# Attention: asking for q and k of the next pair of heads ahead of v of the next four heads

## The chip, the cores and the metric

The kernel runs on one core of one Trainium2 chip. The metric is the device time of one execution in microseconds (us), the median of several runs; lower is better. The engines are named as the profile names them: PE (TensorE, the matrix engine), PEld (its weight loads), DVE (VectorE), ACT (ScalarE), POOL (GpSimd) and SP (SyncE, which here issues the transfers).

## What is computed

One layer of a streaming encoder on 1024 frames of width 1024: a SwiGLU, a mixer with two branches (a gated spatial MLP and an attention), and a second SwiGLU. The change is in the attention, whose 16 heads of width 64 weigh the frames by stick breaking:

```python
z = jnp.einsum('bhtd,bhsd->bhts', qb, kb).astype(jnp.float32) * scale
causal = s_idx < t_idx
log_keep = jnp.where(causal, -jax.nn.softplus(z), 0.0)
log_w = jax.nn.log_sigmoid(z) + lax.cumsum(log_keep, axis=3, reverse=True) - log_keep
w = jnp.where(causal, jnp.exp(log_w), 0.0)
outs.append(jnp.einsum('bhts,bhsd->bhtd', w.astype(vb.dtype), vb))
```

q, k and v are columns of one projection `h @ w_in` of the normed input.

## The kernel before

Each factor of a matmul is kept as two parts, a rounded one and the rest, and a product is three matmuls (lines 67 to 69, `mm3`). A scheduler sets the order on each engine: it takes the instructions in the order in which the program asks for them as their priority, and puts a later one in front when an earlier one has to wait for an operand or for a free buffer. So the order of the calls in `attention` is a ranking, and each engine then runs its own fixed list.

The attention goes through eight pairs of heads. Three kinds of work meet in it:

- `head` (16 times): for each block b of 128 query frames, two matmuls into `z` for up to 512 key frames each (L572, L573), two sigmoids on ACT into `kp` and `bt`, a mask on POOL (L581), a running product on DVE from right to left over `kp` (the scan, L583), a product into `bt` on POOL or DVE (L587), transposes on PE (`tr`, L600), their split into two parts on ACT and DVE (`wt`, L73 and L74), and the product with v (`av`, L607). `kp` has 3 buffers, so block b+3 of a head waits until block b is through.
- `proj_qk` (8 times, once for a pair of heads): q in two halves of 512 frames, then k in two halves, each half 24 matmuls of 512 columns into a PSUM tile `pj` (L67 to L69). Each half of q is then copied into q of the pair's first head and of its second head, the rounded part on ACT and the rest on DVE (`q<-pj`). Tiles `q`, `kh` and `kl` have 3 buffers each, one for a head.
- `proj_v` (4 times, once for four heads, a "group" here): eight products of 24 matmuls of 256 columns into a PSUM tile `pv`, each split into a tile `v`.

`pj` and `pv` are both taken from the PSUM tag `p1`, which has two buffers; the other tags (`p0` with 3 for z, `p2` with 2 for tr, `p3` with 1 for av) hold the other six of the eight banks:

```python
bufs = {"p0": 3, "p1": 2, "p2": 2, "p3": 1}[tag]
```

Heads are numbered 0 to 15, pairs 0 to 7, groups 0 to 3 (heads 0 to 3 are group 0).

Of the kernel before, what the change touches and what calls it, by code (L numbers as in the profile page):

```python
# [32 lines left out]
class Kernel:  # L33
# [483 lines left out]
    def attention(self, ap, ydram):  # L517
        nc, w_in = self.nc, self.a["w_in"][0]

        def proj_v(quad):  # L520
            units = [self.load_cols(w_in, C_VV + quad * 256, kt0, 4, 256) for kt0 in (0, 4)]
            vt = []
            for t in range(NT):
                if quad == 0 and t and self.pending:
                    self.pending.pop(0)()
                half, c = t // 4, (t % 4) * P
                ps = self.psum("p1", "pv")
                for k in range(NK):
                    wh, wl = units[k // 4]
                    hh, hl = (self.h[half][part][:, k, c:c + P] for part in range(2))  # L530
                    self.mm3(ps[:, :256], hh, hl, wh[:, k % 4, :], wl[:, k % 4, :], k == 0, k == NK - 1)
                pool = ap if quad % 2 else self.gp
                v = pool.tile([P, 4, 2, HD], F32R, tag="v", bufs=8, name="v")
                self.split(v[:, :, 0, :], v[:, :, 1, :], ps[:, :256].rearrange("p (h d) -> p h d", h=4))
                vt.append(v)
            return vt

        def proj_qk(pair):
            lo, hi = slice(0, HD), slice(HD, P)
            kl = [ap.tile([P, S], F32R, tag="kl", bufs=3, name="kl") for _ in range(2)]  # L540
            q = [ap.tile([P, S], F32R, tag="q", bufs=3, name="q") for _ in range(2)]
            kh = [ap.tile([P, S], F32R, tag="kh", bufs=3, name="kh") for _ in range(2)]
            wh, wl = self.load_cols(w_in, C_Q + pair * P)
            for half in range(2):
                cs = slice(half * HALF, (half + 1) * HALF)
                ps = self.proj_t("p1", wh, wl, half)
                for e, (own, other) in enumerate(((lo, hi), (hi, lo))):
                    self.split(q[e][own, cs], q[e][other, cs], ps[own, :])
            wh, wl = self.load_cols(w_in, C_K + pair * P)
            for half in range(2):  # L550
                cs = slice(half * HALF, (half + 1) * HALF)
                ps = self.proj_t("p1", wh, wl, half)
                for e, (own, other) in enumerate(((lo, hi), (hi, lo))):
                    self.split(kh[e][own, cs], kl[e][own, cs], ps[own, :])
                    for k in (kh[e], kl[e]):
                        nc.sync.dma_start(out=k[other, cs].bitcast(F32), in_=k[own, cs].bitcast(F32))
            return [(q[e], kh[e], kl[e]) for e in range(2)]
# [62 lines left out]
        qk = {0: proj_qk(0)}  # L620
        npair = NHEAD // 2
        for pair in range(npair):
            for e in range(2):
                head(2 * pair + e, *qk[pair][e], vts[pair // 2])
            if pair % 2 == 1 and pair + 1 < npair:
                vts[pair // 2 + 1] = proj_v(pair // 2 + 1)
            if pair + 1 < npair:
                qk[pair + 1] = proj_qk(pair + 1)


    def gmlp(self, bs):
# [246 lines left out]
```

## Time and profile before

| | |
|---|---|
| median of 3 runs | 2537.75 us (2537.24 to 2537.94) |
| the profiled execution, its own time | 2535.71 us |
| its span, first to last instruction | 2534.0 us |
| busy over the span: PE, PEld, DVE | 2449.6, 2074.1, 1683.1 us |
| busy over the span: ACT, POOL | 1045.2, 351.7 us |
| mean granted clock of PE | 0.986 of full speed |

The span is what the rows below are counted in; the execution's own time is 1.71 us more. Busy time of PE overstates its work, since matmuls are pipelined and one row reaches into the next; the distance from one start to the next is what a matmul takes of PE's time.

### The profile page before, as it was taken

What the parts mean: (1) busy time and instruction counts of PE and PEld (TensorE: products, weight loads), DVE (VectorE), ACT (ScalarE), POOL (GpSimd) and SP (SyncE); (2) the same over time, 40 slices, a digit from 0 to 9 for tenths busy, and PEclk for the clock granted to TensorE, in tenths of its full rate; (3) what the DMA queues carried; (4) which work ended last, traced back from release to release, by engine and by line L of the source; (5) the groups of instructions that cost most, each with busy time, mean ns of one, the idle gap of its engine ahead of it and who ended that gap; (6) DMA issues with size and microseconds to landing.
All of it is one profiled execution on the core that took longest, in us unless ns stands there. A gap on an engine that the chain in (4) does not pass through costs nothing.

```text
span 2534.0 us, 33359 instructions
## 1 busy us (share of the span) xinstructions
PE 2449.6 (97%) x12268; PEld 2074.1 (82%) x12268; DVE 1683.1 (66%) x2579; ACT 1045.2 (41%) x1996; POOL 351.7 (14%) x510
## 2 busy tenths in 40 slices
PE   6999999999999999999999999999979999999998
PEld 5788888788888888888888888888857888887886
DVE  5877787565747888786675555155838777774655
ACT  6333333344545666665422222222334333333444
POOL 4000000000214544444300000000130000000002
PEclk9999999999999999999999999999989999999999
DMA  4553553775421212122121122133445535537653
GB/s 147 175 177 124 176 178 125 292 248 183 159 57 44 67 51 76 46 72 58 39 56 53 47 88 75 58 104 125 133 125 182 174 123 176 181 127 288 235 182 133
DMA packets 257636, 326.73 MB, mean 129 GB/s; under 512 B 15680, under 2 KB 172864, under 8 KB 257472
## 3 DMA queue, kind: packets, MB, share of 16 engines
q1 hardware_dynamic: 257472, 324.60, 39.5%
q8 instruction: 96, 1.57, 0.3%
q14 instruction: 68, 0.56, 0.1%
HBM read 231.74 MB, written 84.41 MB: 125 GB/s over the span
## 4 chain that ended last, share of the span: by engine, by line
PE 85%; DVE 6%; DMA 4%; issue 2%; ACT 2%; POOL 1%; SPq 0%; POOLq 0%; ACTq 0%; DVEq 0%
PE pj L67 7%; PE pj L68 7%; PE pj L69 7%; PE pd L168 7%; PE pd L167 7%; PE pd L166 7%; PE pb L167 5%; PE pb L168 5%; PE pb L166 5%; PE av L607 3%; PE tr L600 2%; PE pv L68 2%; PE pv L69 2%; PE pv L67 2%; PE pe L167 2%
## 5 line engine op out<-in xcount | busy, mean ns | idle before, releaser
L150 ACT CAST wf<-raw 128x512 fp32r<-128x512 f32 x280 | 166.6, 620 | 244.3 <-PE pd L168 108.8
L67 PE MATMUL pj<-h,wf 128*128 128x512 f32 x640 | 254.6, 398 | 5.4 <-DVE q L74 5.4
L151 DVE TENSOR_TENSOR wf<-raw,wf 128x512 fp32r<-128x512 f32 x264 | 177.9, 695 | 119.3 <-ACT wf L150 119.0
L68 PE MATMUL pj<-h,wf 128*128 128x512 f32 x640 | 254.2, 397 | 0.0
L69 PE MATMUL pj<-h,wf 128*128 128x512 f32 x640 | 253.4, 396 | 0.0
L583 DVE TENSOR_TENSOR_SCAN kp<-kp 128x128 f32<-128x128 f32 (+7 forms) x128 | 179.7, 1412 | 37.6 <-POOL kp L581 36.1
L57 DVE TENSOR_TENSOR wf<-raw,wf 128x1024 fp32r<-128x1024 f32 x88 | 110.2, 1252 | 128.5 <-ACT wf L56 128.4
L150 ACT CAST wf<-ws 128x512 fp32r<-128x512 f32 x176 | 108.0, 622 | 190.7 <-DVE ws L159 87.4
L56 ACT CAST wf<-raw 128x1024 fp32r<-128x1024 f32 x88 | 92.7, 1053 | 214.4 <-PE pj L68 117.9
L587 POOL TENSOR_TENSOR bt<-bt,kp 128x512 f32<-128x512 f32 (+4 forms) x128 | 130.3, 1021 | 130.5 <-DVE kp L583 98.0
L67 PEld LDWEIGHTS pj<-h,wf 128*128 128x128 f32 x640 | 122.3, 191 | 31.0 <-DVE q L74 6.8
L67 PE MATMUL pv<-wf,h 128*128 128x256 f32 x512 | 145.2, 286 | 2.5 <-ACT vg L650 2.1
L68 PE MATMUL pv<-wf,h 128*128 128x256 f32 x512 | 145.7, 285 | 0.3 <-DVE wf L57 0.3
L69 PE MATMUL pv<-wf,h 128*128 128x256 f32 x512 | 145.2, 284 | 0.0
L69 PEld LDWEIGHTS pj<-h,wf 128*128 128x128 f32 x640 | 122.0, 191 | 24.6 <-DVE wf L57 0.2
L68 PEld LDWEIGHTS pj<-h,wf 128*128 128x128 f32 x640 | 122.1, 191 | 24.0
L114 POOL TENSOR_TENSOR xn<-x,gain 128x512 f32<-128x512 f32 x12 | 16.7, 1391 | 893.2 <-DVE x L474 601.7
L166 PE MATMUL pb<-T,wf 128*128 128x512 f32 x352 | 137.4, 390 | 0.0
L167 PE MATMUL pb<-T,wf 128*128 128x512 f32 x352 | 137.2, 390 | 0.0
L168 PE MATMUL pb<-T,wf 128*128 128x512 f32 x352 | 136.8, 389 | 0.0
L167 PE MATMUL pd<-wf 128*128 128x512 f32 x344 | 134.7, 392 | 0.2 <-DVE wf L151 0.2
L166 PE MATMUL pd<-wf 128*128 128x512 f32 x344 | 132.8, 393 | 1.9 <-DVE x L463 1.4
(216 smaller groups left out, 6589.3 us busy)
## 6 DMA issues: line engine op xcount, KB each, us to landing
raw<-in_ff_w_down_dram SPq DMA_DIRECT2D x66, 512.0 KB, 6.2
raw<-in_w_in_dram SPq DMA_DIRECT2D x56, 512.0 KB, 3.8
raw<-in_ff_w_gate_dram SPq DMA_DIRECT2D x52, 512.0 KB, 4.3
raw<-in_ff_w_up_dram SPq DMA_DIRECT2D x44, 512.0 KB, 5.5
f_t2t<-as SPq DMA_DIRECT2D x22, 512.0 KB, 4.9
f_a11a<-act SPq DMA_DIRECT2D x44, 256.0 KB, 4.1
f_s2s<-as SPq DMA_DIRECT2D x22, 512.0 KB, 2.9
f_s3s<-as SPq DMA_DIRECT2D x22, 512.0 KB, 5.6
```

Of the source, the lines that this page charges most:

```text
L56: nc.scalar.copy(hi, raw)
L57: (nc.gpsimd if early else nc.vector).tensor_tensor(lo, raw, hi.bitcast(F32), op=ALU.subtract)
L67: mm(ps, lhsT=lh, rhs=rh, start=first, stop=False)
L68: mm(ps, lhsT=lh, rhs=rl, start=False, stop=False)
L69: mm(ps, lhsT=ll, rhs=rh, start=False, stop=last)
L150: self.nc.scalar.copy(f[:, 0, :], src)
L151: (sub or self.nc.vector.tensor_tensor)(f[:, 1, :], src, f[:, 0, :].bitcast(F32), op=ALU.subtract)
L166: mm(ps, lhsT=lh, rhs=rh, start=first, stop=False, skip_group_check=True)
L167: mm(ps, lhsT=lh, rhs=rl, start=False, stop=False, skip_group_check=True)
L168: mm(ps, lhsT=ll, rhs=rh, start=False, stop=last, skip_group_check=True)
L583: nc.vector.tensor_tensor_scan(rev, rev, rev, 1.0, op0=ALU.mult, op1=ALU.bypass)
L587: eng.tensor_tensor(bt[:, :n], bt[:, :n], kp[:, i * HALF + 1:i * HALF + 1 + n], op=ALU.mult)
```

## The change

The two calls at the end of a group change places; nothing else does. It concerns three places of the program, after heads 3, 7 and 11; at the ends of the other pairs only `proj_qk` is called.

```diff
@@ -622,10 +622,10 @@
         for pair in range(npair):
             for e in range(2):
                 head(2 * pair + e, *qk[pair][e], vts[pair // 2])
+            if pair + 1 < npair:
+                qk[pair + 1] = proj_qk(pair + 1)
             if pair % 2 == 1 and pair + 1 < npair:
                 vts[pair // 2 + 1] = proj_v(pair // 2 + 1)
-            if pair + 1 < npair:
-                qk[pair + 1] = proj_qk(pair + 1)
```

Every engine runs the same instructions as before, in another order: PE has 12,268 matmuls in both. The orders part at the end of `proj_qk` of pair 1, while head 1 runs, and what follows comes again with each group.

The first place is PE's list in the middle of head 2, at block 2 (`z_6785`). Before:

```order
L600 MATMUL tr_6553<-ident_66,bt_6537 128x128
L572 MATMUL z_6785<-kh_6608,q_6606 128x384
L573 MATMUL z_6785<-kl_6604,q_6606 128x384
L68 MATMUL pv_7358<-wf_7265,h00_81 128x256
L69 MATMUL pv_7358<-wf_7264,h01_82 128x256
L67 MATMUL pv_7358<-wf_7264,h00_81 128x256
L68 MATMUL pv_7358<-wf_7265,h00_81 128x256
L69 MATMUL pv_7358<-wf_7264,h01_82 128x256
```

And with the change, where `z_6798` and `z_6839` are blocks 3 and 4 of the same head:

```order
L600 MATMUL tr_6553<-ident_66,bt_6517 128x128
L572 MATMUL z_6785<-kh_6608,q_6606 128x384
L573 MATMUL z_6785<-kl_6604,q_6606 128x384
L572 MATMUL z_6798<-kh_6608,q_6606 128x512
L573 MATMUL z_6798<-kl_6604,q_6606 128x512
L600 MATMUL tr_6553<-ident_66,bt_6537 128x128
L600 MATMUL tr_6553<-ident_66,bt_6517 128x128
L600 MATMUL tr_6553<-ident_66,bt_6537 128x128
L607 MATMUL av_6437<-wt_6506,v_5858 128x256
L572 MATMUL z_6839<-kh_6608,q_6606 128x512
L573 MATMUL z_6839<-kl_6604,q_6606 128x512
```

The matmuls of v (`pv`) are gone from head 2; from its first z to the k of pair 2 PE has only 4 matmuls of a projection left among 113.

The second place is DVE's list in head 2 with the change: `q_7264` and `q_7265` are q of heads 4 and 5, `pj_7274` and `pj_7303` the two halves of q of pair 2 in the two buffers of `p1`, and `kp_6913` and `kp_6933` the scans of blocks 6 and 7 of head 2.

```order
L583 SCALAR_TENSOR_TENSOR kp_6913<-kp_6913 128x896
L74 TENSOR_TENSOR wt_6826<-tr_6822,wt_6826 128x384
L587 TENSOR_TENSOR bt_6923<-bt_6923,kp_6913 128x383
L74 TENSOR_TENSOR wt_6883<-tr_6878,wt_6883 128x512
L74 TENSOR_TENSOR q_7265<-pj_7274,q_7265 64x512
L74 TENSOR_TENSOR q_7265<-pj_7303,q_7265 64x512
L583 SCALAR_TENSOR_TENSOR kp_6933<-kp_6933 128x1024
```

Before, the same copies of pair 2 (there `q_7500` and `q_7501`) stood in head 3, each half's two together, behind the scan of its block 6 (`kp_7171`) for the second half:

```order
L583 SCALAR_TENSOR_TENSOR kp_7171<-kp_7171 128x896
L74 TENSOR_TENSOR wt_7084<-tr_7080,wt_7084 128x384
L57 TENSOR_TENSOR wf_8229<-raw_8226,wf_8228 128x1024
L587 TENSOR_TENSOR bt_7181<-bt_7181,kp_7171 128x383
L74 TENSOR_TENSOR wt_7141<-tr_7136,wt_7141 128x512
L74 TENSOR_TENSOR q_7500<-pj_7539,q_7500 64x512
L74 TENSOR_TENSOR q_7501<-pj_7539,q_7501 64x512
```

So with the change both buffers of `p1` are held from the first half of q, in head 1, to the end of head 2.

The third place is PE's list at the first z of head 4 (`z_7642`). Before, it stood right behind k of its pair (`pj_7607`):

```order
L67 MATMUL pj_7607<-h10_83,wf_7570 128x512
L68 MATMUL pj_7607<-h11_84,wf_7570 128x512
L69 MATMUL pj_7607<-h10_83,wf_7571 128x512
L572 MATMUL z_7642<-kh_7502,q_7500 128x128
L573 MATMUL z_7642<-kl_7498,q_7500 128x128
```

With the change the last product of v of the next group stands there:

```order
L67 MATMUL pv_7612<-wf_7412,h10_83 128x256
L68 MATMUL pv_7612<-wf_7413,h10_83 128x256
L69 MATMUL pv_7612<-wf_7412,h11_84 128x256
L572 MATMUL z_7642<-kh_7266,q_7264 128x128
L573 MATMUL z_7642<-kl_7262,q_7264 128x128
```

In front of it all of head 3 is through as well, where before a part of head 3's `tr` and `av` stood behind it.

## Rows read from the trace of the kernel before

**Rows 1.** The page: the span, and each engine's busy time over it.

```profile
span 2534.0 us, 33359 instructions
...
PE 2449.6 (97%) x12268; PEld 2074.1 (82%) x12268; DVE 1683.1 (66%) x2579; ACT 1045.2 (41%) x1996; POOL 351.7 (14%) x510
```

**Rows 2.** The attention: length; busy PE, PEld, DVE, ACT, POOL (count); clock, DMA share, GB/s.

```profile
738.00:1267.00 529.00, 510.42 (x3161) 455.47 (x3159) 406.46 (x460) 321.44 (x693) 234.25 (x384) 0.98 0.22 57
```

**Rows 3.** Timeline of PE: start, duration; in brackets the idle time before.

```profile
737.98 0.56 PE L572 MATMUL z<-kh,q 128*128 128x128 f32 x3
...
763.39 0.79 PE L67 MATMUL pj<-h,wf 128*128 128x512 f32 x1 [3.07 <-DVE q L74]
...
863.76 0.22 PE L572 MATMUL z<-kh,q 128*128 128x128 f32 x1
...
864.58 0.39 PE L67 MATMUL pj<-h,wf 128*128 128x512 f32 x1
...
888.72 0.87 PE L600 MATMUL tr<-ident,bt 128*128 128x128 f32 x3 [3.26 <-DVE wt L74]
...
892.39 0.50 PE L67 MATMUL pj<-h,wf 128*128 128x512 f32 x1 [0.23 <-DVE q L74]
...
989.01 0.31 PE L572 MATMUL z<-kh,q 128*128 128x128 f32 x1
...
1014.14 0.70 PE L600 MATMUL tr<-ident,bt 128*128 128x128 f32 x3 [1.50 <-DVE wt L74]
...
1015.87 0.80 PE L67 MATMUL pj<-h,wf 128*128 128x512 f32 x1 [1.02 <-DVE q L74]
...
1116.22 0.22 PE L572 MATMUL z<-kh,q 128*128 128x128 f32 x1
...
1142.09 0.80 PE L67 MATMUL pj<-h,wf 128*128 128x512 f32 x1 [1.09 <-DVE q L74]
```

**Rows 4.** Two stretches, columns as rows 2; then timeline of PE after the second.

```profile
888.10:891.50 3.40, 2.78 (x12) 2.81 (x13) 3.34 (x3) 2.57 (x8) 0.29 (x1) 0.50 0.66 200
1014.40:1021.20 6.80, 5.78 (x16) 4.22 (x15) 6.46 (x8) 0.84 (x3) 3.51 (x7) 0.50 0.15 31
...
1021.15 0.43 PE L67 MATMUL pj<-h,wf 128*128 128x512 f32 x1
```

**Rows 5.** DVE in the attention by line: busy, mean | idle, releasers; last: one shape.

```profile
L583 DVE TENSOR_TENSOR_SCAN kp<-kp 128x128 f32<-128x128 f32 (+7 forms) x128 | 179.7, 1412 | 37.6 <-POOL kp L581 36.1
L74 DVE TENSOR_TENSOR wt<-tr,wt 128x512 fp32r<-128x512 f32 (+1 forms) x160 | 98.0, 627 | 39.0 <-ACT wt L73 38.3
L587 DVE TENSOR_TENSOR bt<-bt,kp 128x127 f32<-128x127 f32 (+1 forms) x64 | 59.7, 932 | 11.0 <-POOL bt L581 8.3 <-DVE kp L583 0.5
L57 DVE TENSOR_TENSOR wf<-raw,wf 128x1024 fp32r<-128x1024 f32 x29 | 37.5, 1293 | 24.9 <-ACT wf L56 24.9
...
L74 DVE TENSOR_TENSOR q<-pj,q 64x512 fp32r<-64x512 f32 x32 | 21.8, 688 | 10.4 <-ACT q L73 9.8
L74 DVE TENSOR_TENSOR v<-pv,v 128x256 fp32r<-128x256 f32 x32 | 13.2, 412 | 13.2 <-ACT v L73 13.2
...
L583 DVE TENSOR_TENSOR_SCAN kp<-kp 128x1024 f32<-128x1024 f32 x16 | 36.7, 2291 | 1.5 <-POOL kp L581 1.4
```

**Rows 6.** Timeline of PE at full clock, at head 3.

```profile
866.77 0.99 PE L607 MATMUL av<-wt,v 128*128 128x256 f32 x7
867.60 0.93 PE L600 MATMUL tr<-ident,bt 128*128 128x128 f32 x7
868.29 0.48 PE L572 MATMUL z<-kh,q 128*128 128x512 f32 x1
868.60 0.39 PE L573 MATMUL z<-kl,q 128*128 128x512 f32 x1
868.83 0.39 PE L67 MATMUL pj<-h,wf 128*128 128x512 f32 x1
```

**Rows 7.** Transfers: size and median time to landing.

```profile
raw<-in_w_in_dram SPq DMA_DIRECT2D x56, 512.0 KB, 3.8
```

## Prediction

> **What bounds the kernel now.** I read the page's busy times first, then those of the attention alone, then PE's timeline at each idle row there. The span is 2534.0 us [rows 1] and the execution took 2535.71, 2.0 us under the median of 2537.75; a difference of the span is taken over to the median unchanged. From the first z the attention takes 529 us, with PE at 510 us of busy time, DVE at 406 us [rows 2]. So PE's list is nearly always running, DVE has room over the whole stretch, and the order counts for one thing: whether PE always has something ready while a head goes through its chain of ACT, POOL and DVE. Where it had not, PE's timeline shows it: four times, each between the first z of a head and the next matmul of `pj` that needs a buffer of `p1` [rows 3]. At heads 0, 4, 8 and 12 these stretches are 737.98 to 763.39 (25.4 us), 863.76 to 892.39 (28.6), 989.01 to 1015.87 (26.9) and 1116.22 to 1142.09 (25.9), and the wait that ends them is for DVE.
>
> **What the stretches lose.** PE's work in one is its matmuls by what one takes, start to start, at full clock [rows 6]: a matmul of 512 columns 0.23 us (868.60 to 868.83), seven `av` 0.83 (0.119 each), seven `tr` 0.69 (0.099 each); the six small z at head 4 take 0.82 [rows 3], 0.137 each. Counting the lists:
> - head 0: 48 `pj` and 12 wide z, 16 small z, 13 `av`, 18 `tr`: 13.8 + 2.2 + 1.5 + 1.8 = 19.3 us, so 6.1 lost;
> - head 4: 62 wide, 18 small, 33 `av`, 28 `tr`: 14.3 + 2.5 + 3.9 + 2.8 = 23.4, so 5.2 lost;
> - heads 8 and 12 (the same list): 60, 14, 28, 28: 13.8 + 1.9 + 3.3 + 2.8 = 21.8, so 5.1 and 4.1 lost.
>
> The clock adds to it. From 1014.40 to 1021.20 the granted clock was 0.50, the lower level of 1.2 GHz [rows 4], after the idle times of 1.5 and 1.0 us [rows 3]; from 1015.87 to 1021.15 PE ran 12 `pj`, which at full clock are 12 x 0.23 = 2.8 us, so 2.5 us were lost behind the stretch. Heads 0 and 12 have the same tail; at head 4 the lower clock lies inside the stretch (888.1 to 891.5). The ends of the three groups thus lose 5.2 + 7.6 + 6.6 = 19.4 us now. That is all that a better order could win there.
>
> **What the change does.** No instruction is added or removed. Three things move.
>
> First, in head 2 (and 6 and 10, the lists repeat) the matmuls of v are gone, since q of the next pair has both buffers of `p1`. One half of q can give its buffer back only when it has been copied into q of both heads; the second head's tile is the third buffer of `q`, and it is that of head 2, free only when the last z of head 2 is done. DVE's list shows it: the copies into `q_7265` stand behind the scan of block 6. Until then neither k nor v can take a buffer, and PE has only the head's own work. From the first z of head 2 to the first matmul of k: 16 wide matmuls (4 of them `pj`), 14 small z, 44 `av`, 39 `tr`: 3.7 + 1.9 + 5.2 + 3.9 = 14.7 us. In the same stretch DVE has 23 rows, from the scan of block 0 to the copy that frees the first buffer. Eight scans of a head take 8 x 1.412 = 11.3 us; seven, without the widest of 2.29, 9.0. With 9 `wt` at 0.627, 4 `bt` at 0.932, one `wf` at 1.293 and 2 `q` at 0.688 that is 9.0 + 5.6 + 3.7 + 1.3 + 1.4 = 21.0 us [rows 5]. So here PE cannot hide DVE. The floor is DVE without a gap: 21.0 - 14.7 = 6.3 us lost. The ceiling is DVE with the gaps of the four stretches above, which start and end in the same way: head 0 has 18 DVE rows of 19.1 us there (8 scans, 3 `wt`, 2 `bt`, 1 `wf`, 4 copies of q or k), and took 25.4, 6.3 more; head 8 has 21 rows of 19.7 and took 7.2 more. So at most 21.0 + 7.2 = 28.2 us, 13.5 lost. I take 25 us: DVE still has head 1's last rows to do when head 2 starts, so it is fed better than in a cold start, but the widest scan of head 1 stands in front of the first of head 2. 25 - 14.7 = 10.3 us, and 2.5 us of low clock behind it as at head 8: 12.8 us a group. None of it is there now: all of PE's idle rows over a microsecond in the attention lie in the four stretches.
>
> Second, v of the next group comes late, behind k, in heads 3, 7 and 11, and stands in front of the first z of heads 4, 8 and 12 in PE's list. These heads then start when head 3's chain is empty. From `z` to the `pj` that waits, the list has 107 matmuls, 48 `pj` among them, the same counts as at head 0. So each of the three should lose what head 0 loses: 6.1 + 2.5 = 8.6 us, 25.8 together, against 19.4 now: +6.4 us. The bounds: as little as the best of now, 6.6 each (+0.4), or head 4's 28.6 us for this list, 28.6 - 19.3 + 2.5 = 11.8 each (+16).
>
> Third, the transfers. The weights of v are asked for behind k's, between the copies of k within SBUF of pair 1 on SP's queue. A load lands in 3.8 us [rows 7], and PE's list has 96 `pj`, 22 us of work, between k of pair 1 and the first use of v: I cost this at nothing; without that cover it would be the 3.8 us, DVE's `wf` of 1.3 and as much on ACT, about 6 us a group.
>
> **Sum:** 3 x 12.8 + 6.4 = 44.8 us more: 2535.7 + 45 = 2581 for an execution like the profiled one, **2583 us** for the median. With the bounds, 3 x 6.3 + 0.4 = 19 to 3 x (13.5 + 2.5) + 16 = 64: 2557 to 2602.
>
> **A rule weighed.** By head, the work of PE and DVE between the first z of one head and of the next is now 24.6 and 21.4 us (head 2: 8 scans, 9 `wt`, 3 `bt`, 4 `v` on DVE) and 42.5 us and less (head 3). With the change it is 12.9 and 24.1 (head 2: 8 scans, 9 `wt`, 4 `bt`, 1 `wf`, 3 `q`) and 52.4 and less (head 3, with 192 matmuls of v at the 0.119 of an `av` of the same width). If each stretch took just what its busiest engine needs, a group would go from 24.6 + 42.5 = 67.1 to 24.1 + 52.4 = 76.5 us: +9.4, three times +28, 2566 us. The Trainium skill, Perfetto Trace Analysis, section Optimization Strategy, says that where the most-contended engine changes over time, interleaving those regimes may improve performance. This change does the opposite: it pulls a VectorE stretch and a TensorE stretch apart which the order before had mixed, so by that rule it is a loss. No run so far shows it.
>
> **The rivals.**
> - Regimes apart, but no gaps and no lower clock: the 2566 us above. For it: DVE is fed by two heads at the start. Against it: all four stretches took 6 to 7 us more than DVE's rows in them. Chance 0.22.
> - Faster: q and k are ready some 30 us of PE work before head 4 starts, where now k ends at the very z (863.76 is one matmul behind the last `pj`). If the starts of heads 4, 8 and 12 lost their stalls, 19.4 us would come back: 2518 us. It decides if head 2 costs under 6.5 us a group, which is just its floor; and the list puts v ahead of those z, so they don't start early. Chance 0.07.
> - The same: the stall only changes place. PE's and DVE's rows are unchanged in number, so if head 2 loses its floor of 6.3 us and heads 4, 8 and 12 lose nothing, 3 x 6.3 stands against 19.4: 2537 us. Against it speaks head 0, with the same counts and 8.6 us lost. Chance 0.07.
>
> The forecast itself has 0.64, and its bounds hold the first rival too. A measurement here tells about 0.2% (5 us) from no change. Slower 0.86, same 0.07, faster 0.07. The range is 2557 to 2602: it holds most of the first two cases and leaves out the others.
>
> **What would show it.** In the profile after: in each of heads 2, 6 and 10 a stretch of some 25 us in which DVE is above 80% busy and PE idles some 10 us, ended by a `pj` (L67) released by DVE's `q` copy (L74), with a clock of 0.50 around its end; the last waits before `pj` at heads 4, 8 and 12 like that at 763.39; the distance between the first z of heads 4 and 8, now 125.3 us, near 141 (12.8 more in head 6, 8.6 in place of 5.2 at head 4). I am wrong in the size if head 2's stretch is near 21 or 28 us, and in the mechanism if PE's idle time there ends on something else, or if heads 4, 8 and 12 start without a stall.

## The result, and the profile after

The change makes the kernel slower: 2578.06 us (2574.76 to 2583.04, 6 runs) against 2536.65 us (2534.14 to 2537.94, 6 runs) for the kernel before on the same chip, a ratio of 1.0163 with a 95% interval of 1.0152 to 1.0174. That is 41.4 us, where 45 were forecast. The profiled execution of after took 2576.55 us with a span of 2574.8, 40.8 us more than the span of before [rows 1].

The page of after: the span, and each engine's busy time.

```profile
span 2574.8 us, 33346 instructions
...
PE 2469.4 (96%) x12268; PEld 2085.6 (81%) x12268; DVE 1684.0 (65%) x2579; ACT 1046.0 (41%) x1996; POOL 365.4 (14%) x510
```

The work is the same: as many matmuls and DVE rows as before, and DVE's busy time within a microsecond. PE's busy time grew by 20 us without one matmul more. So part of the loss is idle time, and part is that PE ran the same matmuls slower.

Now the stretches, in the columns of [rows 2]: length; busy time of PE, PEld, DVE, ACT, POOL with counts; granted clock, DMA share, GB/s. First the attention, then heads 2, 6 and 10 from the first `z` to the first `pj` of k, then heads 4, 8 and 12 from the first `z` to the `pj` that waits, and last two pieces of heads 2 and 4.

```profile
736.90:1306.40 569.50, 529.09 (x3160) 465.99 (x3159) 408.50 (x460) 321.05 (x691) 247.78 (x384) 0.95 0.21 53
798.03:825.70 27.67, 20.19 (x115) 16.96 (x113) 25.53 (x28) 19.95 (x45) 16.38 (x26) 0.81 0.16 39
937.92:965.83 27.91, 20.48 (x116) 17.17 (x115) 25.58 (x28) 20.05 (x46) 16.38 (x26) 0.82 0.16 38
1077.24:1105.69 28.45, 20.88 (x117) 17.40 (x116) 25.97 (x29) 20.80 (x49) 16.99 (x27) 0.87 0.17 41
876.93:902.67 25.74, 22.20 (x110) 18.06 (x108) 20.03 (x21) 16.90 (x38) 16.75 (x23) 0.88 0.26 73
1017.03:1042.78 25.75, 21.92 (x109) 17.90 (x108) 20.04 (x21) 16.89 (x38) 16.60 (x23) 0.93 0.26 73
1158.16:1183.90 25.74, 20.50 (x109) 16.64 (x108) 20.04 (x21) 16.89 (x38) 17.17 (x23) 0.99 0.26 72
804.50:811.30 6.80, 4.03 (x19) 3.57 (x18) 6.60 (x8) 3.63 (x8) 4.18 (x8) 0.50 0.27 78
902.67:906.90 4.23, 4.23 (x10) 3.36 (x11) 4.17 (x7) 0.38 (x1) 2.02 (x4) 0.50 0.00 0
```

The whole loss lies in the attention: from the first `z` to the last `av` it takes 569.5 us, where it took 527.4 (737.98 to 1265.39), 42.1 more. Heads 2, 6 and 10 are the new rows: 27.7, 27.9 and 28.5 us in which DVE is over 91% busy and PE is idle for 7.5. (113, 114 and 116 matmuls start in them: head 2 has 4 of `pj`, head 6 has 5 and head 10 has 7, so the lists do not repeat to the matmul. PE's counts take in one or two more that reach over an edge.)

PE's timeline of after in heads 2 and 4: start, duration, what, and in brackets the idle time before and what ended it.

```profile
798.03 0.22 PE L572 MATMUL z<-kh,q 128*128 128x128 f32 x1
...
802.46 0.50 PE L572 MATMUL z<-kh,q 128*128 128x512 f32 x1 [1.13 <-ACT bt L576]
...
803.64 0.55 PE L600 MATMUL tr<-ident,bt 128*128 128x128 f32 x3 [0.45 <-POOL bt L587]
...
807.67 1.22 PE L607 MATMUL av<-wt,v 128*128 128x256 f32 x4 [2.77 <-DVE wt L74]
...
815.34 0.56 PE L607 MATMUL av<-wt,v 128*128 128x256 f32 x3 [0.64 <-DVE wt L74]
...
820.57 0.62 PE L607 MATMUL av<-wt,v 128*128 128x256 f32 x3 [2.49 <-DVE wt L74]
...
825.70 0.40 PE L67 MATMUL pj<-h,wf 128*128 128x512 f32 x1
...
876.93 0.22 PE L572 MATMUL z<-kh,q 128*128 128x128 f32 x1
...
896.07 0.74 PE L607 MATMUL av<-wt,v 128*128 128x256 f32 x4 [1.11 <-DVE wt L74]
...
902.67 0.79 PE L67 MATMUL pj<-h,wf 128*128 128x512 f32 x1 [1.58 <-DVE q L74]
```

In head 2 PE's idle time, 7.5 us in five pieces, stands in front of the head's own matmuls, mostly `av` that waits for DVE's `wt`. The `pj` that the prediction looked at, at 825.70, has no idle time in front of it. At head 4 the wait does end on a `pj` and on the q copy, as before at 763.39 and 892.39 [rows 3].

DVE's timeline of after through the same head 2.

```profile
798.00 0.69 DVE L74 TENSOR_TENSOR wt<-tr,wt 128x512 fp32r<-128x512 f32 x1 [0.20 <-ACT wt L73]
798.97 0.69 DVE L74 TENSOR_TENSOR wt<-tr,wt 128x512 fp32r<-128x512 f32 x1 [0.28 <-ACT wt L73]
799.90 2.29 DVE L583 TENSOR_TENSOR_SCAN kp<-kp 128x1024 f32<-128x1024 f32 x1 [0.24 <-POOL kp L581]
802.23 0.68 DVE L74 TENSOR_TENSOR q<-pj,q 64x512 fp32r<-64x512 f32 x1
802.94 0.93 DVE L583 TENSOR_TENSOR_SCAN kp<-kp 128x128 f32<-128x128 f32 x1
803.79 0.70 DVE L587 TENSOR_TENSOR bt<-bt,kp 128x511 f32<-128x511 f32 x1
804.42 1.30 DVE L57 TENSOR_TENSOR wf<-raw,wf 128x1024 fp32r<-128x1024 f32 x1
...
818.57 1.35 DVE L587 TENSOR_TENSOR bt<-bt,kp 128x255 f32<-128x255 f32 x1
...
822.82 1.22 DVE L587 TENSOR_TENSOR bt<-bt,kp 128x383 f32<-128x383 f32 x1
823.97 0.68 DVE L74 TENSOR_TENSOR wt<-tr,wt 128x512 fp32r<-128x512 f32 x1
824.67 1.30 DVE L74 TENSOR_TENSOR q<-pj,q 64x512 fp32r<-64x512 f32 x2
```

The rows up to 802.94 are head 1's and a copy of q: the first scan of head 2 starts 4.9 us after its first `z`. From that scan to the end of the first q copy, half of the last row (some 825.3), are 22.4 us. DVE does one row after the other there, with idle pieces under 0.7 us.

### The profile page after: what moved, and what is told of

It is laid out like the page before. It is cut to its first block, busy times and chain, and to the rows that moved or that the text cites. A ratio compares the mean times of both kernels' runs of the same rounds, so it can differ in the third digit from the quotient of the medians.

```text
span 2574.8 us, 33346 instructions
## 1 busy us (share of the span) xinstructions
PE 2469.4 (96%) x12268; PEld 2085.6 (81%) x12268; DVE 1684.0 (65%) x2579; ACT 1046.0 (41%) x1996; POOL 365.4 (14%) x510
## 4 chain that ended last, share of the span: by engine, by line
PE 81%; DVE 7%; DMA 5%; issue 3%; POOL 2%; ACT 2%; SPq 0%; POOLq 0%; ACTq 0%; DVEq 0%
PE pj L67 6%; PE pj L68 6%; PE pj L69 6%; PE pd L168 6%; PE pd L167 6%; PE pd L166 6%; PE pb L167 5%; PE pb L168 5%; PE pb L166 5%; PE pv L68 2%; PE pv L67 2%; PE pv L69 2%; PE av L607 2%; PE tr L600 2%; DMA raw<-in_ff_w_down_dram 2%
## 5 line engine op out<-in xcount | busy, mean ns | idle before, releaser
L583 DVE TENSOR_TENSOR_SCAN kp<-kp 128x128 f32<-128x128 f32 (+7 forms) x128 | 183.6, 1442 | 58.1 <-POOL kp L581 56.4
L607 PE MATMUL av<-wt,v 128*128 128x256 f32 (+1 forms) x640 | 120.0, 297 | 25.1 <-DVE wt L74 21.7
L69 PEld LDWEIGHTS pj<-h,wf 128*128 128x128 f32 x640 | 122.1, 191 | 25.7 <-DVE wf L57 1.1
L575 ACT ACTIVATE kp<-z 128x512 f32<-128x512 f32 (+1 forms) x192 | 96.4, 507 | 99.2 <-PE z L573 52.0
```

The source lines that it names most:

```text
L69: mm(ps, lhsT=ll, rhs=rh, start=False, stop=last)
L583: nc.vector.tensor_tensor_scan(rev, rev, rev, 1.0, op0=ALU.mult, op1=ALU.bypass)
L607: nc.tensor.matmul(av[:, ac + o0:ac + 256], lhsT=lhs, rhs=wt[:, part, jj * 256:jj * 256 + 256 - o0], start=j0 + jj + part == 0, stop=diag ...
```

## The experiments

The theory is the prediction's: both buffers of `p1` wait for the third buffer of `q`, which empties PE's list in heads 2, 6 and 10, where DVE then sets the length. Each kernel ran beside the kernel before on the same chip; its median there is 2534.3 to 2535.9 us. A word ahead of all of them: the scheduler orders every variant anew, so none of them changes one thing alone, and each was read by its trace as well as by its time.

**one_place.** The calls change places after head 11 only.

```diff
+            if pair + 1 < npair and pair == 5:
+                qk[pair + 1] = proj_qk(pair + 1)
             if pair % 2 == 1 and pair + 1 < npair:
                 vts[pair // 2 + 1] = proj_v(pair // 2 + 1)
-            if pair + 1 < npair:
+            if pair + 1 < npair and pair != 5:
                 qk[pair + 1] = proj_qk(pair + 1)
```

> The two calls change places at the end of group 2 alone (after head 11); the other two ends stay as before. My account (each end of a group pays for itself: some 13 us in head 10, where PE has nothing but the head's own work, and 1 to 2 us more at head 12): 41/3, so 12 to 16 us over before, about 2551. Rival, a loss that comes from the groups shifting against each other and builds up from one to the next: well under 10 us.

2548.99 us (2547.31 to 2551.53), ratio 1.0055 (1.0039 to 1.0072): 13.1 us, a third of 41.4. Its row for head 10 (stretches as above):

```profile
1049.35:1074.80 25.45, 19.35 (x119) 16.12 (x117) 22.87 (x27) 20.15 (x46) 16.59 (x26) 0.93 0.15 42
```

One place of three costs a third of the whole, so neither the whole order nor anything at the start is needed for it. By the count at the end of this section, 9.8 us of it lie in heads 10 and 11 and 2.9 in heads 12 and 13.

**after_q4 and before_q4.** A fourth buffer of `q`, paid for with one buffer of `y`, in the changed kernel and in the kernel before.

```diff
-            q = [ap.tile([P, S], F32R, tag="q", bufs=3, name="q") for _ in range(2)]
+            q = [ap.tile([P, S], F32R, tag="q", bufs=4, name="q") for _ in range(2)]
...
-                    y = ap.tile([P, HALF], F32, tag="y", bufs=2, name="y")
+                    y = ap.tile([P, HALF], F32, tag="y", bufs=1, name="y")
```

> The change with a fourth buffer for q (y gets one buffer for two, to make room). q of the next pair then need not wait for the last z of head 2, p1 comes free, and PE's list has the 48 matmuls of k (11 us) in head 2. My account (the wait for a buffer of q, which holds p1, empties head 2): most of head 2's 13 us goes, in three places: 2530 to 2550 us, 28 us or more under the change. Rival (the cost is the late start of heads 4, 8 and 12 behind v, which stays): within 8 us of the change, 2570 or more.

> The kernel before with the same fourth buffer of q and one of y. Control for the run above. My account: the waits for q's buffer at heads 0, 4, 8 and 12 (5 to 8 us each) get shorter too, since k's first half need not wait: 2515 to 2532 us, faster than before. Rival (the buffer of q matters only with the change): 2537 within 5 us. If this one gains as much as the change does, the buffer is worth something but doesn't explain the loss.

The changed kernel with it takes 2547.17 us, ratio 1.0049 (1.0034 to 1.0064): 30.9 us less, which is within what was expected. But the kernel before takes 2514.25 us (2511.58 to 2517.2) with it, ratio 0.9915 (0.9901 to 0.9930), 21.7 us faster than it was: the version that beats both. Between the two the swap still costs 33 us, so the simple account, that q's buffer is all of it, is wrong. The attention of before_q4:

```profile
735.28:1238.50 503.22, 497.62 (x3161) 448.54 (x3159) 407.88 (x460) 320.72 (x691) 247.36 (x384) 1.00 0.24 60
```

At a clock of 1.00 PE is idle for 5.6 us in all. The stretches of heads 0, 4, 8 and 12, 25.4 to 28.6 us in [rows 3], are 15.6 to 16.6 there, counted to the same, 49th, `pj`. The stalls of the kernel before at these heads went with the same buffer.

The changed kernel's gain is this same gain, and not the one that was expected. By the count at the end of this section with the fourth buffer it lost 29.3 us less in the other heads, where both orders have their stalls (0, 4, 8 and 12 and what follows them), and 39.7 us in heads 2, 3, 6, 7, 10 and 11, where it had lost 41.0. So its time came out as forecast while the loss that the swap brought stayed.

PE's timeline of after_q4, in heads 2, 3 and 10:

```profile
796.45 0.50 PE L67 MATMUL pj<-h,wf 128*128 128x512 f32 x1 [2.87 <-DVE q L74]
...
813.89 0.40 PE L69 MATMUL pj<-h,wf 128*128 128x512 f32 x1
...
825.69 1.22 PE L607 MATMUL av<-wt,v 128*128 128x256 f32 x4 [2.88 <-DVE wt L74]
...
828.83 0.56 PE L67 MATMUL pv<-wf,h 128*128 128x256 f32 x1
...
1060.60 0.80 PE L67 MATMUL pj<-h,wf 128*128 128x512 f32 x1 [4.25 <-DVE q L74]
```

The 48 `pj` of k now stand in head 2 (first `z` at 790.76), where the change had 4. But from the last of them at 813.89 to the first `pv` at 828.83, in head 3, there is again no projection on PE. By the code the holder of `p1` is now k, whose copies go into `kh` and `kl`, which still have three buffers; that these are what it waits for was the reason for the next pairs of runs. And k starts behind a wait for a q copy all the same, of 2.87 us at 796.45 and of 4.25 us at 1060.60, in head 10: with four buffers, by the code, q of head 5 takes the tile of head 1, and q of head 13 that of head 9, which are in use until those heads' last `z`.

**after_y1.** The changed kernel with one buffer of `y` and nothing else, one run.

```diff
-                    y = ap.tile([P, HALF], F32, tag="y", bufs=2, name="y")
+                    y = ap.tile([P, HALF], F32, tag="y", bufs=1, name="y")
```

> The change with one buffer of y and three of q, to see what the lost buffer of y costs by itself. My account: y is written 32 times, 16 us apart on average, and its transfer out takes 2.4 us: within 4 us of the change, 2574 to 2582.

2577.47 us, against 2578.06: in the changed order the buffer that the fourth q was paid with costs nothing that shows, and the 30.9 us are q's. In the order before this was not run.

**after_b4 and before_b4.** Four buffers for `q`, `kh` and `kl`; the room comes from `y`, `bt` and `wt`.

```diff
-KPB, BTB, WTB, DVB = 3, 6, 3, 4
+KPB, BTB, WTB, DVB = 3, 4, 2, 4
...
-            kl = [ap.tile([P, S], F32R, tag="kl", bufs=3, name="kl") for _ in range(2)]
+            kl = [ap.tile([P, S], F32R, tag="kl", bufs=4, name="kl") for _ in range(2)]
...
```

> The change with four buffers each for q, kh and kl; to make room bt has 4 for 6, wt 2 for 3 and y 1 for 2. Now neither q nor k of the next pair waits for head 2, p1 is never held, and PE's list has matmuls of k and v in head 2. My account (the swap costs only because copies wait for a buffer and hold p1): within 8 us of the same buffers without the swap (the next run). Rival, from the run with a fourth q buffer alone, where the swap still cost 33 us: the order itself, v late and in front of the next group's z, costs some 30 us whatever the buffers.

> The kernel before with the same buffers (q, kh, kl 4; bt 4, wt 2, y 1). Control for the run above. PE's list is filled evenly, as with the fourth q buffer (2514 us); what bt and wt lose may cost some of it: 2505 to 2535 us by both accounts.

2570.03 us, ratio 1.0131 (1.0116 to 1.0146), and 2572.04 us, ratio 1.0139 (1.0123 to 1.0154). Here the swap costs nothing (2 us the other way). But the control missed what was expected of it: with fewer buffers of `bt` and `wt` both attentions are slow, 558.7 and 562.4 us. An effect of the order may be covered by that, so another way to find the room was tried.

**after_w4 and before_w4.** Four buffers for `q`, `kh` and `kl` again; the room comes from `y` and from the weights' tag `wf`, 6 buffers to 4.

```diff
-        hi, lo = (self.wp.tile([P, 1024], F32R, tag="wf", bufs=6, name="wf") for _ in range(2))
+        hi, lo = (self.wp.tile([P, 1024], F32R, tag="wf", bufs=4, name="wf") for _ in range(2))
...
-            kl = [ap.tile([P, S], F32R, tag="kl", bufs=3, name="kl") for _ in range(2)]
+            kl = [ap.tile([P, S], F32R, tag="kl", bufs=4, name="kl") for _ in range(2)]
```

> The change with four buffers each for q, kh and kl again, room made elsewhere: y 1 for 2 and the split weights wf 4 for 6, bt and wt as before (the pair with 4 bt and 2 wt was slow with and without the swap, so it showed no more than that the swap cost nothing there). PE's list in heads 2 and 3 is filled with k and v. My account: within 8 us of the next run, while the pair with a fourth buffer of q alone was 33 us apart. Rival (v behind k costs whatever the buffers): 25 us or more over the next run.

> The kernel before with the same buffers (q, kh, kl 4; y 1; wf 4). Control. PE's list in the attention is that of the fourth q buffer alone (2514 us); fewer wf buffers may cost both SwiGLU layers some time: 2514 to 2560 us by both accounts.

2583.03 us, ratio 1.0190 (1.0173 to 1.0207), and 2570.26 us, ratio 1.0139 (1.0122 to 1.0156). Both lose time outside the attention, where fewer buffers of weights are the likely reason (not traced). The attention itself:

after_w4, the attention:

```profile
744.58:1253.40 508.82, 491.69 (x3089) 439.61 (x3087) 400.20 (x459) 319.27 (x690) 231.96 (x384) 0.99 0.23 58
```

before_w4, the same:

```profile
746.17:1238.50 492.33, 483.27 (x3089) 435.32 (x3087) 405.27 (x459) 319.72 (x690) 247.27 (x384) 1.00 0.24 60
```

These lengths can be compared with each other, and not with those above: 3089 matmuls stand in them and not 3160, since 72 `pj` that elsewhere run before the last `av` (16.6 us of work at 0.23 each) come behind it here. The swap costs 12.8 us of the time and 16.5 of the attention, neither of the two expected values. PE's idle rows of over 0.3 us within these windows add up to 16.4 us against 8.7, and the largest of after_w4 is a wait that before_w4 has not, on its PE timeline:

```profile
933.89 0.79 PE L67 MATMUL pj<-h,wf 128*128 128x512 f32 x1 [4.41 <-DVE q L74]
```

A `pj` waits for a q copy even with four buffers, as in after_q4; a second such wait, at 804.93, took 2.88 us. What is left of the 16.5 us was not traced to rows. PE's list did answer as the theory says: in after_w4, v follows right behind k, in head 2:

```profile
822.36 0.40 PE L69 MATMUL pj<-h,wf 128*128 128x512 f32 x1
822.59 0.28 PE L67 MATMUL pv<-wf,h 128*128 128x256 f32 x1
```

From the first `z` of head 2 to that of head 3, PE has 4 projection matmuls with the change, 48 of k with a fourth buffer of `q`, and 48 of k and 63 of v with four buffers of all three.

**after_dvb9 and before_dvb9.** If DVE sets the length of heads 2, 6 and 10, taking rows from it must shorten them. All products into `bt` go to POOL.

```diff
-KPB, BTB, WTB, DVB = 3, 6, 3, 4
+KPB, BTB, WTB, DVB = 3, 6, 3, 9
```

> The change with all products into bt on POOL (none on DVE), which takes 4 rows of 0.93 us, 3.7 us, from DVE in each head. My account (DVE's rows set the length of head 2's stretch, 27.9 us after the change): the stretch shortens by 3 to 4 us, three times, and the distance to the next run is 28 to 34 us instead of 41. Rival (the chain of one block through ACT, POOL and DVE sets it, not DVE's sum): POOL's rows are longer than DVE's, the stretch is as long or longer, and the distance is 41 or more.

> The kernel before with all products into bt on POOL. Control for the run above; both accounts: within 8 us of before, since DVE has room over the whole attention and only the stretches at heads 0, 4, 8 and 12 could gain or lose a microsecond or two each.

2577.60 us, ratio 1.0156 (1.0139 to 1.0173), and 2532.11 us (10 runs), ratio 0.9982 (0.9972 to 0.9991). The stretches of after_dvb9:

```profile
797.74:822.68 24.94, 18.14 (x109) 14.76 (x107) 21.56 (x23) 18.85 (x44) 21.31 (x27) 0.93 0.17 43
937.71:962.47 24.76, 17.77 (x106) 14.51 (x104) 21.61 (x23) 18.51 (x43) 21.44 (x28) 0.86 0.18 43
1077.60:1102.34 24.74, 17.74 (x105) 14.53 (x104) 21.59 (x23) 18.51 (x43) 21.39 (x28) 0.86 0.18 43
```

DVE's busy time there fell by 4.0 us (25.5 to 21.6) and the stretch by 2.7 to 3.7, while POOL's rose from 16.4 to 21.3. That speaks for DVE, and against POOL, as what sets the length. It is not a clean test, since PE's list there is 6 to 12 matmuls shorter too (0.6 to 1.9 us of work). The time of the kernel as a whole did not follow: heads 4, 8 and 12 took 26.5 us in place of 25.7, with longer waits before `pj` (3.3 us in place of 1.6 at head 4), and from first `z` to first `z` heads 5, 9 and 13 took 2.2, 3.3 and 3.0 us more; the kernel before gained 3.6 us by the same edit. The distance of the pair, 45.5 us, missed what was expected and lies where the rival put it (41 or more), though not for the rival's reason, since the stretch is shorter and not longer.

**after_vp2.** In the changed kernel, v of groups 1 to 3 goes to the other PSUM tag of two buffers, so that it needs no buffer of `p1`.

```diff
-                ps = self.psum("p1", "pv")
+                ps = self.psum("p2" if quad else "p1", "pv")
```

> The change with v of groups 1 to 3 in PSUM tag p2 (which it then shares with tr) in place of p1. In PE's list head 2 is as empty as with the change, but head 4's first z no longer stands behind v: v comes between the z of head 4, so its stall is filled. My account (13 us a group in head 2, 8 us at heads 4, 8 and 12): the 13 stay, the 8 go: 41 over before less 19 to 25, about 2552 to 2560 us. Rival (v in front of head 4's first z is what costs): back to 2540 or less.

2590.31 us (2589.71 to 2592.88), ratio 1.0223 (1.0208 to 1.0238): slower still, and both expectations were wrong. Head 2, and then head 4 from its first `z` to the first `pj` behind v:

```profile
796.61:824.32 27.71, 20.42 (x114) 17.05 (x113) 25.65 (x28) 19.82 (x45) 16.38 (x26) 0.82 0.16 39
855.84:905.16 49.32, 42.90 (x310) 39.15 (x308) 28.09 (x36) 24.76 (x54) 16.95 (x26) 0.97 0.16 44
```

Head 2 is as long as it was. v did not fill it; it came as one block inside head 4, where it shares `p2` with head 4's own `tr`, whose chain stood still meanwhile. That v has no buffer of `p1` is therefore not shown to be what keeps it out of head 2. Here it could as well be the `p2` that it shares, its weights, or its rank behind k; the rank alone did not keep it out in after_w4. Had v filled the idle 7.5 us of head 2, the first theory would be shown outright; as it went, this run neither shows nor refutes it.

**The cost of the swap by buffers and by place.** In the last two columns: what the attention lost in the kernel before's order, then in the changed one. Lost is the distance from the first `z` of a head to that of the next, less PE's work in it at full clock, at the prediction's prices for a matmul (0.119 us for `pv`, as wide as `av`). The work so counted differs by up to 1 us between kernels that do the same, so the sums are no better than that.

| buffers | kernel before's order | changed order | cost of the swap | lost in heads 2, 3, 6, 7, 10, 11 | lost in the other heads |
|---|---|---|---|---|---|
| q, kh, kl 3 | 2536.65 | 2578.06 | 41.4 us | 4.5, 41.0 | 28.5, 33.1 |
| q 4 | 2514.25 | 2547.17 | 32.9 us | 0.6, 39.7 | 8.3, 3.8 |
| q, kh, kl 4; wf 4 | 2570.26 | 2583.03 | 12.8 us | 0.3, 23.0 | 13.7, 8.0 |
| q, kh, kl 4; bt 4, wt 2 | 2572.04 | 2570.03 | -2.0 us | 39.3, 6.3 | 28.0, 58.1 |

The swap's cost lies in heads 2, 3, 6, 7, 10 and 11: 36.5 us of the 41 that this count gives for it. There a fourth buffer of `q` took away 1.3 us, close to what the count can tell, and four of all three (with `wf` 4) took 18. The 8.7 us that before_w4 lost in heads 14 and 15, behind which its 72 `pj` now come, hide a part of the swap's cost in its 12.8 us; after_w4 lost 3.4 there.

## Why the prediction was right, point by point

**Slower, and where.** Right: three new stretches in heads 2, 6 and 10, places of equal cost as far as one of the three was run alone (one_place), and nothing outside the attention.

**Heads 2, 6 and 10.** The forecast was 12.8 us a group, 38.4 in all. The stretches less their work at full clock (14.7, 14.9 and 15.4 us by their lists) are 13.0, 13.0 and 13.1 us; the half clock reaches past the end only in the third, to 1108.3, some 1.3 us lost. Together 40.4. The size held, and two of its parts did not. The 25 us taken for the stretch were 27.7 to 28.5, at the ceiling of 28.2 and once past it; DVE's first scan of head 2 came 4.9 us behind the first `z`. And the 2.5 us of low clock behind the stretch were hardly there: the clock was at 0.50 inside it, from 804.5 to 811.3 and from 821.6 to 825.0. In parts, head 2 lost 7.5 us of idle time (27.67 - 20.19) and some 5.5 us in which PE was busy longer than its work at full clock (20.19 - 14.7), where 10.3 and 2.5 were forecast. Of the 5.5 some 3.7 are the clock: half of the 4.03 and 3.41 us that PE was busy in the two pieces at 0.50. That the longer stretch and the missing tail nearly cancel is luck, and so in part is the total. For DVE as what sets the length speak its timeline, with no idle piece over 0.7 us from the first scan of head 2 on, and after_dvb9.

**What ends PE's idle time there.** This step failed, by the prediction's own words: it was to end on a `pj` released by the q copy, and it ends on `av` and `z` that wait for DVE's `wt` and ACT's `bt`. Each engine runs a fixed list. The copy of q that comes late was already reckoned with when PE's list was written: the scheduler put the first `pj` behind the head's work, so when the chip comes to it the copy has just been done, and what waits is the head's own chain. The missing buffer shows in what is not in the list, and only the DVE rows in front of the waiting matmuls show in the trace.

**Heads 4, 8 and 12.** Forecast 8.6 us each by head 0's list, 25.8 in all. The stretches are 25.74, 25.75 and 25.74 us, head 0's 25.4 and 0.3, so 6.4 lost in each; the tails at half clock (902.67 to 906.9 and the like) lost 2.1, 1.7 and 1.45 more. 24.5 in all, 5.1 more than the 19.4 of before, where +6.4 was forecast. Equal counts in the list gave equal times.

**The sum.** 40.4 + 5.1 = 45.5 by these rows; measured 42.1 in the attention. The difference lies in what the prediction put at nothing: "None of it is there now", because all of PE's idle rows over a microsecond lay elsewhere. By the table's count heads 2, 3, 6, 7, 10 and 11 lost 4.5 us in the kernel before, some of it in idle pieces of 0.3 to 0.6 us (0.63 at 799.77). The first `z` of heads 4 and 8 are 140.1 us apart (876.93 to 1017.03), forecast 141. The transfers cost nothing that shows: in the attention of after PE has one idle piece of over 0.2 us that ends on weights, of 0.29 us at 1301.30.

**The first rival and the rule.** The 2566 us was 12 us short, but not in the heads that it was worked out for. It gave head 2 24.1 us from its first `z` to that of head 3, and heads 2, 6 and 10 took 24.4, 24.8 and 24.3 us (798.03 to 822.45 in the first); heads 2 and 3 together, and their like, grew by 10.2, 8.7 and 10.9 us where it gave 9.4 each, 29.8 us for its 28. What it left out are the heads before them: from the first `z` of heads 0, 4 and 8 to that of heads 2, 6 and 10 it took 4.0, 6.2 and 3.1 us more, most of it because PE's list has 4.4, 3.0 and 3.0 us more work there, q of the next pair in v's place. The forecast's stretch of 27.7 us is longer than 24.4 because it runs on to the `pj` inside head 3. The Trainium skill, Perfetto Trace Analysis, section Optimization Strategy, holds that interleaving regimes with different busiest engines may improve performance: this pair of traces agrees, since the stretch with DVE at 25.5 of 27.7 us is one that the order before had mixed with v, and pulling it apart came with 41 us. The order is not the whole of it, though: with four buffers of q and k the same swap cost 12.8 us and -2.0.

**What stays open.** The account of q's buffer is right for the list and not proved for the time. That too few buffers keep the projections out of head 2 is shown by what came into it, 4, 48 and 111 matmuls. But with a fourth buffer of `q` those heads lost 39.7 us and not 41.0, the stall having moved behind k; and with four of all three they still lost 23.0, where waits of 2.88 and 4.41 us for q copies are the part that was traced. How much belongs to each of the three tags is not shown either: each variant has its own order, fewer `bt`, `wt` or `wf` change the kernel too, and with `bt` 4 and `wt` 2 the loss changed heads with the order.

## What to carry to other kernels

When a projection's PSUM buffers can be given back only into a tile that a running head still holds, look at what the engine lists contain in that time: work asked for behind it is missing from the list, and here no wait in heads 2, 6 and 10 named the buffer. Before changing the order of such requests, see whether one more buffer of the tile that is waited for takes the stall away: here it was worth 21.7 us in the order that was already better, more than the 19.4 us that the prediction held a better order could win. And test the buffer in both orders, and count the loss by place: the changed order gained 30.9 us by the buffer, as forecast, and nearly all of it came from stalls that the order before had too.

## What the runs showed of the hardware

PE's granted clock fell to 0.50, its lower level of 1.2 GHz, inside a head. In head 2 it did so from 804.5 on, behind idle pieces of 1.13 and 0.45 us and 0.4 us before the one of 2.77 begins; in head 6 it fell at the same place, 6.5 us behind the first `z` (944.45, behind pieces of 1.14 and 0.45 us and before the one of 2.63 that ends at 947.79). In head 10, where the first piece was 0.68 us, it fell some 4 us later (1087.81, 0.7 us behind the piece of 2.89 that ends at 1087.12). So three heads with nearly the same list did not lose the clock at the same point, and each lost it inside the head, not only behind it.

Some DVE rows took longer than others with more elements: `bt` of 255 columns 1.35 us at 818.57, of 511 columns 0.70 at 803.79. POOL's timeline of after, in head 2:

```profile
800.00 2.28 POOL L581 TENSOR_SCALAR_AFFINE_SELECT bt<-bt 128x128 f32<-128x128 f32 x1
802.24 0.29 POOL L581 TENSOR_SCALAR_AFFINE_SELECT kp<-kp 128x128 f32<-128x128 f32 x1
...
818.55 1.09 POOL L587 TENSOR_TENSOR bt<-bt,kp 128x512 f32<-128x512 f32 x1 [1.69 <-DVE kp L583]
...
822.53 1.09 POOL L587 TENSOR_TENSOR bt<-bt,kp 128x512 f32<-128x512 f32 x1 [2.22 <-DVE kp L583]
```

Both long DVE rows start while a product runs on POOL and end 0.3 to 0.4 us after it (819.92 against 819.64, 824.04 against 823.62). The other way round, the mask at 800.00 takes 2.28 us in place of 0.29: it begins 0.1 us into DVE's scan of 2.29 us and ends with it. The Trainium skill, SBUF — State Buffer, section Who interferes with whom, says that a DVE instruction with two inputs in SBUF contends with a GpSimd instruction that reads SBUF; these rows agree, with some 0.9 us for the `bt` row of 255 columns and 2.0 for the mask. The price of the `bt` row is read against the same row in head 4, where POOL ran masks and no product beside it:

```profile
896.40 0.48 DVE L587 TENSOR_TENSOR bt<-bt,kp 128x255 f32<-128x255 f32 x1
```
